# Column mean of an 8192 x 8192 matrix on one core: half-partition loads, slabs by row, and the last slab but one added on VectorE

## The chip, the cores and the metric

The kernel runs on one core of a Trainium2 chip. The metric is the time that the device takes for one execution, in microseconds (us). Lower is better.

## What is computed

```python
def setup_inputs():
    return {"x": np.random.randn(8192, 8192).astype(np.float32)}

def reference(x):
    return np.mean(x, axis=0)
```

The input is 268 MB of float32 and is read once; the output is one row of 8192 numbers. Each output is the sum of a column of 8192 rows, times 1/8192.

## The kernel before, in words

On-chip memory has 128 partitions. The matrix is cut into 64 slabs of 128 rows. Slabs 0 to 61 are taken as 31 pairs (`n_pairs`), one row of each slab per partition; slabs 62 and 63 are the tail.

**Pairs.** A tile `pair` holds 2 x 8192 columns on 128 partitions, and a pool has three such buffers (lines 41 and 93). In a pair's source, partition p holds the matrix rows 2p and 2p + 1 of the pair's 256 rows, which lie one behind the other in memory: 64 KB without a gap (line 94). Most pairs are one DMA of 8.4 MB. Pair 0 is cut after its first 2048 columns (`FIRST`), and the last three pairs (`BY_ROW = 3`, numbers 28 to 30) come in two DMAs, one for each of the two rows of a partition (lines 95 to 98). All loads are issued by SyncE (SP), in program order, onto one queue.

VectorE does two adds per pair (lines 99 to 102). The first adds the running sum, which stands in the first half of the pair before (`before`), to the first half of the new pair; this frees the older buffer. The second adds the new pair's second half. So the running sum moves along from buffer to buffer. A load into a buffer waits until the first add of the pair behind that buffer's old content is done. Each load signals through a semaphore, and the program has eight of these for loads, used in turn, so that a DMA also waits until the one eight places before it has landed.

**Tail.** The tail tile takes the pool's next buffer: slab 62 (`slab`) in its first half and slab 63 (`last`) in its second. Slab 62 comes in columns 0 to 4095 and 4096 to 7679 (`SPLIT`); its last 512 columns come as two loads of 120 and 8 partitions (`ROWS`, lines 112 and 113). Slab 63 comes in seven pieces of falling width (`PIECES`, line 116).

**The sum over partitions.** TensorE multiplies with a matrix of ones (128 x 32), which sums a column over the 128 partitions. The columns are dealt to PSUM banks: `WIDE` (three of 2048 and one of 1024 columns, each as four groups of a quarter) and `NARROW` (four of 256 columns). A bank collects from up to three sources: the running sum (`before`), slab 62 and slab 63. The first matmul of a bank has `start=True`, the last `stop=True`.

The second add of pair 30 is done in four parts of 2048 columns (lines 120 and 121), and VectorE adds slab 62's last 2048 columns to the last of these (line 123). The other three quarters of slab 62 go to TensorE (line 135). TensorE's order is written out by hand: for wide bank 0, 1, 2 the running sum and slab 62; wide bank 3 and the narrow banks from the running sum; then slab 63 for wide banks 0 to 3 (`close`, lines 139 and 140), each followed by a scaling on ScalarE (ACT); then slab 63 for the narrow banks, with scalings in turn on VectorE and ScalarE (lines 150 to 157). Three DMAs write the output: one from GpSimd (POOL) for the first 6144 columns, two from SP for the next 1024 and the last 1024.

The order on every engine is the order in the program (`manual_schedule`); no planner moves work.

Of the kernel before, what the change touches and what calls it, by code (L numbers as in the profile page):

```python
# [1 line left out]

# [4 lines left out]

F32 = mybir.dt.float32
ADD = mybir.AluOpType.add
GROUPS = 4  # L10

WIDE = (2048, 2048, 2048, 1024)
NARROW = (256, 256, 256, 256)
PIECES = (4096, 2048, 1024, 512, 256, 160, 96)
FIRST = 2048
BY_ROW = 3

ROWS = 120  # L20
SPLIT = 7680


@with_exitstack
def kernel(
    ctx: ExitStack,
    tc: tile.TileContext,
    x: bass.AP,
    out: bass.AP,
):  # L30
    nc = tc.nc
    P = nc.NUM_PARTITIONS
    R, C = x.shape
    n_slabs = R // P
    n_pairs = n_slabs // 2 - 1
    N0 = sum(WIDE)
    assert n_slabs % 2 == 0 and n_pairs >= 4 and N0 + sum(NARROW) == sum(PIECES) == C
    inv_r = 1.0 / float(R)

    const_pool = ctx.enter_context(tc.tile_pool(name="const", bufs=1))  # L40
    pair_pool = ctx.enter_context(tc.tile_pool(name="pair", bufs=3))
    psum_pool = ctx.enter_context(
        tc.tile_pool(name="acc", bufs=1, space=bass.MemoryType.PSUM)
    )
    res_pool = ctx.enter_context(tc.tile_pool(name="res", bufs=1))


    ctx.enter_context(tc.manual_schedule())

    ones = const_pool.tile([P, 32], F32)  # L50
    nc.gpsimd.memset(ones, 1.0)  # L51

    wide, lo = [], 0
    for n, w in enumerate(WIDE):
        bank = psum_pool.tile([P, w // GROUPS], F32, name=f"wide{n}", tag=f"wide{n}")
        wide.append((lo, w, bank))
        lo += w
    narrow = []
    for n, w in enumerate(NARROW):
        bank = psum_pool.tile([P, 512], F32, name=f"narrow{n}", tag=f"narrow{n}")  # L60
        narrow.append((lo, w, 32 * n, bank))
        lo += w

    def mm(dst, src, **flags):
        nc.tensor.matmul(out=dst, lhsT=ones, rhs=src, skip_group_check=True, **flags)  # L65

    def fold_wide(n, src, **flags):
        lo, w, bank = wide[n]
        q = w // GROUPS
        for g in range(GROUPS):  # L70
            a = lo + g * q
            mm(bank[32 * g : 32 * g + 32, :], src[:, a : a + q], **flags)

    def fold_narrow(n, src, lo, hi, **flags):
        at, _, g, bank = narrow[n]
        mm(bank[g : g + 32, lo - at : hi - at], src[:, lo:hi], **flags)

    def scaled(dst, src, eng):
        if eng == "act":
            nc.scalar.mul(out=dst, in_=src, mul=inv_r)  # L80
        else:
            nc.vector.tensor_scalar(  # L82
                out=dst, in0=src, scalar1=inv_r, scalar2=None, op0=mybir.AluOpType.mult
            )

    def add(dst, a, b):
        nc.vector.tensor_tensor(out=dst, in0=a, in1=b, op=ADD)  # L87

    before = None
    for k in range(n_pairs):
        pair = pair_pool.tile([P, 2 * C], F32, tag="pair")
        src = x[2 * P * k : 2 * P * (k + 1), :].rearrange("(p j) c -> p (j c)", j=2)
        cut = FIRST if k == 0 else C if k >= n_pairs - BY_ROW else 2 * C
        for lo, hi in ((0, cut), (cut, 2 * C)):
            if lo < hi:
                nc.sync.dma_start(out=pair[:, lo:hi], in_=src[:, lo:hi])  # L98
        if before is not None:
            add(pair[:, 0:C], pair[:, 0:C], before[:, 0:C])  # L100
        if k < n_pairs - 1:
            add(pair[:, 0:C], pair[:, 0:C], pair[:, C : 2 * C])
        before = pair


    tail = pair_pool.tile([P, 2 * C], F32, tag="pair")
    r = (n_slabs - 2) * P
    slab, last = tail[:, 0:C], tail[:, C : 2 * C]
    parts = [(lo, lo + w) for lo, w, _ in wide[:3]] + [(wide[3][0], C)]
    for lo, hi in ((0, C // 2), (C // 2, SPLIT)):  # L110
        nc.sync.dma_start(out=slab[:, lo:hi], in_=x[r : r + P, lo:hi])
    for a, b in ((0, ROWS), (ROWS, P)):
        nc.sync.dma_start(out=slab[a:b, SPLIT:C], in_=x[r + a : r + b, SPLIT:C])
    lo = 0
    for w in PIECES:
        nc.sync.dma_start(out=last[:, lo : lo + w], in_=x[r + P : R, lo : lo + w])
        lo += w


    for lo, hi in parts:  # L120
        add(before[:, lo:hi], before[:, lo:hi], before[:, C + lo : C + hi])
    lo, hi = parts[3]
    add(before[:, lo:hi], before[:, lo:hi], slab[:, lo:hi])

    rw = res_pool.tile([P, 3 * 512], F32, name="rw")
    r3 = res_pool.tile([P, WIDE[3] // GROUPS], F32, name="r3")
    row = res_pool.tile([1, C - N0], F32, name="row")

    def close(n):
        fold_wide(n, last, start=False, stop=True)  # L130
        scaled(rw[:, n * 512 : (n + 1) * 512] if n < 3 else r3, wide[n][2], "act")

    for n in range(3):
        fold_wide(n, before, start=True, stop=False)
        fold_wide(n, slab, start=False, stop=False)
    fold_wide(3, before, start=True, stop=False)
    for n, (lo, w, _, _) in enumerate(narrow):
        fold_narrow(n, before, lo, lo + w, start=True, stop=False)
    for n in range(4):
        close(n)  # L140
    W3 = 3 * GROUPS * 512
    nc.gpsimd.dma_start(  # L142
        out=out[0:W3].rearrange("(n g w) -> g n w", g=GROUPS, w=512),
        in_=rw.rearrange("(g r) (n w) -> g r n w", r=32, w=512)[:, 0],
    )
    nc.sync.dma_start(
        out=out[W3:N0].rearrange("(g w) -> g w", g=GROUPS),
        in_=r3.rearrange("(g r) w -> g r w", r=32)[:, 0],
    )
    for n, (lo, w, g, bank) in enumerate(narrow):  # L150
        if n < 3:
            fold_narrow(n, last, lo, lo + w, start=False, stop=True)
        else:
            cut = C - PIECES[-1]
            fold_narrow(n, last, lo, cut, start=False, stop=True)
            fold_narrow(n, last, cut, C, start=False, stop=True)
        scaled(row[0:1, lo - N0 : lo - N0 + w], bank[g : g + 1, 0:w], "act" if n % 2 else "dve")
    nc.sync.dma_start(out=out[N0:C], in_=row)


# [1 line left out]
_INS = ['x']  # L162
_OUTS = [((8192,), 'float32')]


# [23 lines left out]
```

## Time and profile before

| | |
|---|---|
| time, median of 3 runs | 629.22 us (628.69 to 629.66) |
| span of the profiled execution | 627.3 us |
| difference of the two | 1.9 us |
| read from memory | 268.44 MB, 428 GB/s over the span |
| load queue, share of 16 DMA engines' span | 99.2% |
| VectorE busy | 533.5 us (85%) |
| TensorE busy | 13.0 us (2%) |
| one add of 128 x 8192 | 8.692 us |
| one add of 128 x 2048 | 2.286 us |
| matmul records | 106, two for each matmul of the program |

The profiled execution has no time of its own apart from its span; the unprofiled runs' median lies 1.9 us above it. The profile names engines PE (TensorE), DVE (VectorE), ACT (ScalarE), POOL (GpSimd) and SP (SyncE). A group of instructions is shown with its line, its engine, its operation, the tiles that it writes and reads, its shape and its count; in square brackets stands how long the engine was idle before it and what ended that idle time. A table of stretches gives for each window the busy time of every engine, the clock granted to TensorE, the busy share of the DMA engines and the GB/s that they moved.

### The profile page before, as it was taken

Reading aid. Unit: us, or ns where it says so; the run is one execution under the profiler, and the core shown is the slowest. Engines: PE = TensorE matmul, PEld = TensorE weight load, DVE = VectorE, ACT = ScalarE, POOL = GpSimd, SP = SyncE. Lnnn points to the kernel's source line nnn. Section 1 sums busy time; section 2 is a strip of 40 time slices with the busy share of each in tenths; the row PEclk is TensorE's granted clock in tenths of the full one; section 3 lists DMA queues with packets and bytes.
Section 4 is the critical chain, followed back from the end, with each engine's and each line's share of the span. In section 5 each row is a group of like instructions: output and inputs, shape, how many; then the busy total and the mean of one; then the engine's idle time right before and its main releaser. Section 6 shows DMA issues by size and latency. Waiting matters only on the chain.

```text
span 627.3 us, 451 instructions
## 1 busy us (share of the span) xinstructions
PE 13.0 (2%) x106; PEld 3.8 (1%) x106; DVE 533.5 (85%) x67; ACT 4.2 (1%) x7; POOL 1.0 (0%) x6
## 2 busy tenths in 40 slices
PE   0000000000000000000000000000000000000016
PEld 0000000000000000000000000000000000000001
DVE  0538988889888899888898888988889888899994
ACT  0000000000000000000000000000000000000001
POOL 0000000000000000000000000000000000000000
PEclk9999999999999999999999999999999999999999
DMA  9999999999999999999999999999999999999997
GB/s 414 396 460 401 468 401 468 401 451 418 443 426 430 439 426 443 418 451 410 460 405 464 401 468 401 468 402 468 401 468 401 468 401 468 401 433 435 435 421 287
DMA packets 6548, 268.50 MB, mean 428 GB/s; under 512 B 900, under 2 KB 1160, under 8 KB 1553
## 3 DMA queue, kind: packets, MB, share of 16 engines
q1 hardware_dynamic: 6497, 268.45, 99.2%
q0 software_dynamic: 48, 0.02, 0.0%
q8 instruction: 1, 0.02, 0.0%
q14 instruction: 2, 0.02, 0.0%
HBM read 268.44 MB, written 0.03 MB: 428 GB/s over the span
## 4 chain that ended last, share of the span: by engine, by line
DMA 77%; DVE 22%; PE 0%; issue 0%; SPq 0%; ACT 0%; DVEq 0%
DMA pair<-in_x_dram 72%; DVE pair L87 22%; DMA tail<-in_x_dram 5%; PE narrow L65 0%; SPq L98 0%; PE wide L65 0%; ACT row L80 0%; DVEq L87 0%
## 5 line engine op out<-in xcount | busy, mean ns | idle before, releaser
L87 DVE TENSOR_TENSOR pair<-pair 128x8192 f32<-128x8192 f32 (+1 forms) x64 | 530.4, 8292 | 85.2 <-DMA pair<-in_x_dram 84.1
L65 PE MATMUL wide<-pair,ones 128*32 128x512 f32 (+1 forms) x32 | 4.8, 679 | 610.8 <-DVE pair L87 610.8
L65 PE MATMUL wide<-tail,ones 128*32 128x512 f32 (+1 forms) x56 | 7.7, 634 | 0.7 <-DMA tail<-in_x_dram 0.7
L82 DVE TENSOR_SCALAR row<-narrow 1x256 f32<-1x256 f32 x2 | 0.8, 416 | 6.2 <-PE narrow L65 6.1
L80 ACT ACTIVATE rw<-wide 128x512 f32<-128x512 f32 x3 | 1.8, 597 | 619.5 <-PE wide L65 619.5
L65 PEld LDWEIGHTS wide<-pair,ones 128*32 128x32 f32 x32 | 1.1, 134 | 613.5 <-issue 610.3
L87 DVE TENSOR_TENSOR pair<-pair,tail 128x2048 f32<-128x2048 f32 x1 | 2.3, 2292 | 0.0
L65 PEld LDWEIGHTS wide<-tail,ones 128*32 128x32 f32 x56 | 1.7, 119 | 6.1 <-issue 3.1
L142 POOL DMA_DIRECT2D out_dram<-rw x1 | 0.7, 695 | 622.7 <-ACT rw L80 622.7
L80 ACT ACT_TABLE_LOAD x1 | 1.3, 1283 | 0.7 <-PEq L173 0.7
L65 PE MATMUL narrow<-tail,ones 128*32 128x256 f32 (+2 forms) x10 | 1.2, 346 | 0.0
L80 ACT ACTIVATE row<-narrow 1x256 f32<-1x256 f32 x2 | 0.8, 376 | 0.4 <-PE narrow L65 0.2
L65 PEld LDWEIGHTS narrow<-tail,ones 128*32 128x32 f32 x10 | 0.6, 108 | 0.8 <-DMA tail<-in_x_dram 0.6
L65 PE MATMUL narrow<-pair,ones 128*32 128x256 f32 x8 | 0.6, 379 | 0.0
L80 ACT ACTIVATE r<-wide 128x256 f32<-128x256 f32 x1 | 0.4, 384 | 0.2 <-PE wide L65 0.2
L65 PEld LDWEIGHTS narrow<-pair,ones 128*32 128x32 f32 x8 | 0.3, 110 | 0.2
L51 POOL MEMSET ones<- 128x32 f32 x1 | 0.1, 124 | 0.3 <-POOLq L173 0.3
L173 POOL MEMSET const-float32-0.0<- 128x1 f32 x1 | 0.1, 98 | 0.2 <-issue 0.2
L173 POOL MEMSET const-float32-1.0<- 128x1 f32 x1 | 0.1, 98 | 0.0
L173 POOL MEMSET const-bfloat16-1.0<- 128x1 bf16 x1 | 0.1, 98 | 0.0
L173 POOL MEMSET const-uint8-127<- 128x1 uint8 x1 | 0.1, 98 | 0.0
## 6 DMA issues: line engine op xcount, KB each, us to landing
pair<-in_x_dram SPq DMA_DIRECT2D x6, 4096.0 KB, 25.8
pair<-in_x_dram SPq DMA_DIRECT2D x1, 7168.0 KB, 21.1
tail<-in_x_dram SPq DMA_DIRECT2D x2, 2048.0 KB, 19.2
tail<-in_x_dram SPq DMA_DIRECT2D x1, 1792.0 KB, 24.0
pair<-in_x_dram SPq DMA_DIRECT2D x1, 1024.0 KB, 4.7
tail<-in_x_dram SPq DMA_DIRECT2D x1, 1024.0 KB, 30.2
tail<-in_x_dram SPq DMA_DIRECT2D x1, 512.0 KB, 28.8
pair<-in_x_dram SPq DMA_DIRECT2D x27, 29.8
```

Of the source, the lines that this page charges most:

```text
L51: nc.gpsimd.memset(ones, 1.0)
L65: nc.tensor.matmul(out=dst, lhsT=ones, rhs=src, skip_group_check=True, **flags)
L80: nc.scalar.mul(out=dst, in_=src, mul=inv_r)
L82: nc.vector.tensor_scalar(out=dst, in0=src, scalar1=inv_r, scalar2=None, op0=mybir.AluOpType.mult)
L87: nc.vector.tensor_tensor(out=dst, in0=a, in1=b, op=ADD)
L142: nc.gpsimd.dma_start(out=out[0:W3].rearrange("(n g w) -> g n w", g=GROUPS, w=512), in_=rw.rearrange("(g r) (n w) -> g r n w", r=32, w=512 ...
L173: nc = _bacc.Bacc("TRN2", target_bir_lowering=False, num_devices=1)
```

## The change

- Pairs 0 to 24 are loaded in two DMAs, partitions 0 to 63 and 64 to 127; pair 0 in four, since it is still cut after 2048 columns.
- The last six pairs (25 to 30, `BY_ROW = 6`) are loaded slab by slab: partition p holds row p of the first slab and row p of the second. Pair 30 (`BY_HALF = 1`) comes in four loads of 4096 columns, and each of its two adds is done in two halves of 4096 columns.
- Slab 62 comes in two loads of 4096 columns on all 128 partitions. VectorE adds all of it to the running sum, in four parts of 2048 columns, and TensorE does not read it.
- Slab 63 comes in eight pieces; the first 4096 columns are now two pieces.
- The last narrow bank (256 columns) becomes two, of 160 and 96; the fifth narrow bank takes the PSUM place of wide bank 0 once that has been scaled. Its scaling is on VectorE.
- TensorE's 53 matmuls become 42, in another order: bank 0 from the running sum and from slab 63, then bank 1 the same, then bank 2, bank 3 and the narrow banks from the running sum, then slab 63 for the rest.

```diff
-NARROW = (256, 256, 256, 256)
-PIECES = (4096, 2048, 1024, 512, 256, 160, 96)
+NARROW = (256, 256, 256, 160, 96)
+PIECES = (2048, 2048, 2048, 1024, 512, 256, 160, 96)
 FIRST = 2048
-BY_ROW = 3
-
-ROWS = 120
-SPLIT = 7680
+BY_ROW = 6
+BY_HALF = 1
...
-    for n, w in enumerate(NARROW):
-        bank = psum_pool.tile([P, 512], F32, name=f"narrow{n}", tag=f"narrow{n}")
-        narrow.append((lo, w, 32 * n, bank))
-        lo += w
+    def open_narrow():
+        lo = N0
+        for n, w in enumerate(NARROW):
+            tag = f"narrow{n}" if n < GROUPS else "wide0"
+            bank = psum_pool.tile([P, 512], F32, name=f"narrow{n}", tag=tag)
+            narrow.append((lo, w, 32 * (n % GROUPS), bank))
+            lo += w
...
-        src = x[2 * P * k : 2 * P * (k + 1), :].rearrange("(p j) c -> p (j c)", j=2)
-        cut = FIRST if k == 0 else C if k >= n_pairs - BY_ROW else 2 * C
-        for lo, hi in ((0, cut), (cut, 2 * C)):
-            if lo < hi:
-                nc.sync.dma_start(out=pair[:, lo:hi], in_=src[:, lo:hi])
-        if before is not None:
-            add(pair[:, 0:C], pair[:, 0:C], before[:, 0:C])
-        if k < n_pairs - 1:
-            add(pair[:, 0:C], pair[:, 0:C], pair[:, C : 2 * C])
+        r = 2 * P * k
+        step = C
+        if k >= n_pairs - BY_ROW:
+            if k >= n_pairs - BY_HALF:
+                step = C // 2
+            for j in range(2):
+                for lo in range(0, C, step):
+                    nc.sync.dma_start(
+                        out=pair[:, j * C + lo : j * C + lo + step],
+                        in_=x[r + j * P : r + j * P + P, lo : lo + step],
+                    )
+        else:
+            src = x[r : r + 2 * P, :].rearrange("(p j) c -> p (j c)", j=2)
+            for lo, hi in ((0, FIRST), (FIRST, 2 * C)) if k == 0 else ((0, 2 * C),):
+                for a in (0, P // 2):
+                    b = a + P // 2
+                    nc.sync.dma_start(out=pair[a:b, lo:hi], in_=src[a:b, lo:hi])
+        for lo in range(0, C, step):
+            if before is not None:
+                add(pair[:, lo : lo + step], pair[:, lo : lo + step], before[:, lo : lo + step])
+        for lo in range(0, C, step):
+            add(pair[:, lo : lo + step], pair[:, lo : lo + step], pair[:, C + lo : C + lo + step])
...
-    for lo, hi in ((0, C // 2), (C // 2, SPLIT)):
+    for lo, hi in ((0, C // 2), (C // 2, C)):
         nc.sync.dma_start(out=slab[:, lo:hi], in_=x[r : r + P, lo:hi])
-    for a, b in ((0, ROWS), (ROWS, P)):
-        nc.sync.dma_start(out=slab[a:b, SPLIT:C], in_=x[r + a : r + b, SPLIT:C])
...
     for lo, hi in parts:
-        add(before[:, lo:hi], before[:, lo:hi], before[:, C + lo : C + hi])
-    lo, hi = parts[3]
-    add(before[:, lo:hi], before[:, lo:hi], slab[:, lo:hi])
+        add(before[:, lo:hi], before[:, lo:hi], slab[:, lo:hi])
...
-    for n in range(3):
-        fold_wide(n, before, start=True, stop=False)
-        fold_wide(n, slab, start=False, stop=False)
+    fold_wide(0, before, start=True, stop=False)
+    close(0)
+    fold_wide(1, before, start=True, stop=False)
+    close(1)
+    fold_wide(2, before, start=True, stop=False)
+    open_narrow()
     fold_wide(3, before, start=True, stop=False)
     for n, (lo, w, _, _) in enumerate(narrow):
         fold_narrow(n, before, lo, lo + w, start=True, stop=False)
-    for n in range(4):
-        close(n)
+    close(2)
+    close(3)
...
-        if n < 3:
-            fold_narrow(n, last, lo, lo + w, start=False, stop=True)
-        else:
-            cut = C - PIECES[-1]
-            fold_narrow(n, last, lo, cut, start=False, stop=True)
-            fold_narrow(n, last, cut, C, start=False, stop=True)
+        fold_narrow(n, last, lo, lo + w, start=False, stop=True)
```

## The prediction, made before the changed kernel had run

> **What bounds the kernel now.** I read the page's engine and DMA lines first, then VectorE's timeline, then a table of stretches, then the timeline of the last 20 us.
>
> ```profile
> PE 13.0 (2%) x106; PEld 3.8 (1%) x106; DVE 533.5 (85%) x67; ACT 4.2 (1%) x7; POOL 1.0 (0%) x6
> ...
> q1 hardware_dynamic: 6497, 268.45, 99.2%
> ...
> HBM read 268.44 MB, written 0.03 MB: 428 GB/s over the span
> ```
>
> The load queue keeps the 16 DMA engines busy for 99.2% of 627.3 us; VectorE (85%) is second. So a load that was merely late in being issued is not what costs time here; only the pace of the engines, and the two ends, can.
>
> ```profile
> 41.89 17.42 DVE L87 TENSOR_TENSOR pair<-pair 128x8192 f32<-128x8192 f32 x2 [10.76 <-DMA pair<-in_x_dram]
> 61.35 17.42 DVE L87 TENSOR_TENSOR pair<-pair 128x8192 f32<-128x8192 f32 x2 [2.04 <-DMA pair<-in_x_dram]
> ...
> 409.74 17.42 DVE L87 TENSOR_TENSOR pair<-pair 128x8192 f32<-128x8192 f32 x2 [1.85 <-DMA pair<-in_x_dram]
> 429.86 17.42 DVE L87 TENSOR_TENSOR pair<-pair 128x8192 f32<-128x8192 f32 x2 [2.70 <-DMA pair<-in_x_dram]
> ...
> 545.65 69.98 DVE L87 TENSOR_TENSOR pair<-pair 128x8192 f32<-128x8192 f32 x11 [1.89 <-DMA pair<-in_x_dram]
> 615.66 2.29 DVE L87 TENSOR_TENSOR pair<-pair,tail 128x2048 f32<-128x2048 f32 x1
> ```
>
> A line is a pair: two adds, 17.42 us, then a wait for the next landing. Starts lie 19.30 us apart in the steady part (8.39 MB each, 435 GB/s), a little more in the first six pairs (61.35 - 41.89 = 19.46; 0.9 us too much in all), and 20.12 us once, at 429.86. From 545.65 on VectorE never waits and ends at 617.95.
>
> ```profile
> 41.80:545.60 503.80, 0.00 (x0) 0.00 (x0) 451.98 (x52) 0.00 (x0) 0.00 (x0) 1.00 1.00 432
> ...
> 611.50:614.50 3.00, 3.00 (x28) 0.92 (x24) 3.00 (x2) 0.00 (x0) 0.00 (x0) 1.00 1.06 352
> ```
>
> The last two columns are the DMA share and GB/s. In 611.5 to 614.5 the engines are as busy as ever and move 352 GB/s: (432 - 352) x 3.0 us = 240 KB too little, 0.56 us. This is where the 120-row and 8-row loads (L113) run.
>
> ```profile
> 618.01 0.64 PE L65 MATMUL wide<-pair,ones 128*32 128x256 f32 x8 [1.66 <-DVE pair L87]
> 618.46 0.61 PE L65 MATMUL narrow<-pair,ones 128*32 128x256 f32 x8
> ...
> 622.82 0.64 PE L65 MATMUL wide<-tail,ones 128*32 128x256 f32 x8 [0.17 <-DMA tail<-in_x_dram]
> 623.44 1.16 PE L65 MATMUL narrow<-tail,ones 128*32 128x256 f32 x10
> ...
> 624.14 0.88 ACT L80 ACTIVATE row<-narrow 1x256 f32<-1x256 f32 x2 [0.23 <-PE narrow L65]
> ...
> 625.09 0.27 SPq L158 DMA_DIRECT2D out_dram<-row  x1
> ```
>
> TensorE is done with the pair at 619.1 and then waits for pieces of the last slab; from 622.8 everything follows the last landings.
>
> **Durations.** The DMA packet records of this execution, read one by one: 64 KB packets take 2.418 us (median of 3,456), 32 KB 1.213, 16 KB 0.611, 14 KB 0.535, 8 KB 0.309, 2 KB 0.084, and each engine's closing packet of a load 0.009. A full load is eight packets on each engine. The sum is made against the profiled execution, span 627.3; the median of the runs, 629.22, lies 1.9 us above it, and I carry that 1.9 over.
>
> **The change, part by part.**
>
> *Pairs 0 to 24 in two loads of 64 partitions.* If 64 partitions still spread over 16 engines (four packets each) at 2.418 us, only 26 more closing packets come in: 26 x 0.009 = +0.23. SP issues 26 more DMAs at 0.33 to 0.43 us, hidden: a slot's load is issued some 10 us before the stream reaches it (issue at 50.61, data from 61.3). Each half sits behind the other on one queue, and the wait for VectorE stands on the first half alone. What is not in the trace is 16 engines that write into 64 partitions only. Lower bound: nothing, or a gain up to the 0.9 us that the first pairs lose, since no row excludes that. Upper bound: the nearest row where rows and engines do not pair as in a full load, L113. Its 256 KB are 0.59 us of work at 435 GB/s and the stretch loses 0.56 us besides, so about twice the time; twice 19.30 for 25 pairs is +483 us. L113 may be slow for its odd row counts or its size instead: the 512-column piece of the last slab, also 2 KB packets, on 128 rows, shows 0.084 throughout. I take the low end, because four 64 KB packets per engine are nearest in size and queue to the 3,456 that ran at 2.418.
>
> [...]
>
> *Pairs 25 to 27 by row as well.* 16 packets of 1.213 for 8 of 2.418, one more closing packet: 3 x 0.073 = +0.22.
>
> *Pair 30 in quarters.* 32 x 0.611 for 16 x 1.213 and two closings: +0.16.
>
> *Slab 62 in two plain halves.* 16 x 0.611 = 9.78 for 8 x (0.611 + 0.535 + 0.084) = 9.84: -0.06, and the slow stretch goes, -0.56 (between 0, if it belongs to the place, and -0.56). One engine had been spared L113's share and now gets 0.61 back; it ends 0.25 to 0.5 us ahead of the others and 1.27 ahead of the last one (622.85 against 624.12), so 0.66 of cover is left.
>
> *Last slab's first piece in two:* 16 x 0.309 for 8 x 0.611: +0.07. The last four pieces are as before, each issued some 9 us before its data (its semaphore's earlier load, eight back, lands by 613.8).
>
> *VectorE.* It gains whole adds on slab 62 (three more 128x2048 of 2.29), and starts pairs 25 to 27 half a pair earlier. Replayed with 8.70 per add and 4.42 for 128x4096 (interpolated between 2.29 and 8.69): pair 24 lands at 487.7, adds run without a gap to 610.8, slab 62's four to 620.0, against 617.95. Four 256-column and five narrow matmuls then take 1.1 (rows at 618.01 to 619.07): 621.1. Wide 2's last four, on a piece that now lands at 621.54, take 0.43 to 0.86 (four weight loads step by 0.86 us at 610 and by 0.43 at 614), so 622.4 at the latest, before the 1024-column piece at 622.77. Counted from 621.1 the cover is 0.8 us; what VectorE is later than that goes one to one into the end.
>
> *Data order on TensorE.* Wide 0 and wide 1 are now closed before the pair's later parts are begun, so wide 1's start on the pair (VectorE's release at 615.4) waits behind wide 0's close on the last slab's first piece, about 616.7 (the 4096 columns land at 619.12, less 2.4 for 2048), and wide 2's start (617.7) behind the second piece at 619.12. ScalarE's scalings come earlier by this, and all of it ends before 621.1's work can: 0.
>
> *Eleven matmuls fewer* (twelve on slab 62 go, one narrow start comes; the trace counts each twice): they ran before 616, in the shade of the loads, 0. *Last scaling:* 96 columns on VectorE (under the 0.416 of 256) for 0.376 on ACT: 0 to -0.15, I take -0.1.
>
> *Instruction fetch.* The records show one 8 KB fetch of the instruction queue at 414.0 us; right after it one of the 16 engines lands 0.7 us late (the 20.12 step), and stays late to the end. More DMAs on SP may bring a second: 0 to +0.75, I take +0.3.
>
> Sum: 0.23 + 0.22 + 0.16 - 0.06 - 0.56 + 0.07 - 0.1 + 0.3 = +0.3, so 627.6 span, 629.5 us. Own range of this case, with the bounds above: 628.0 to 631.0.
>
> **The rivals.**
>
> *B, the lost steps go.* If halves read without the slow first pairs (-0.9) and the fetch falls where no engine is late (-0.8 and not +0.3), the end is 629.5 - 2.0 = 627.5. For it: both losses are in the trace and neither belongs to the work. Against: nothing in the change aims at the fetch.
>
> *C, two engines share one way into the 64 partitions, all along.* Place: every half load of pairs 0 to 24. Price: 25 x 19.3 = +483, 1112 us. It decides from the point where partners run in step, and engines do: they land within 0.3 us of each other. For it: L113's stretch. Against: every other packet of the trace runs at its engine's own pace, and that one odd load is the only witness.
>
> *D, they share but fall out of step.* Once one of two partners is a half load behind, they write to different halves and both run at full pace; the trailing one ends a half load (19.30 / 2 = 9.7 us) late: 639, and up to 649 if that takes twice as long to form.
>
> *E, VectorE ends too late.* If its replay is 1.5 us short, 0.8 of it covered, and TensorE stays at its slower pace (four 256-column, five narrow and four 512-column matmuls, some 0.9 more), about +1.5: 631. For it: its eleven adds in a row end only 5 us before the last landings. Against: the adds' length varies by 0.01 us.
>
> **How the numbers follow.** 0.2%, 1.26 us, is about what can be told from no change. Forecast A 0.42 (of it 0.05 faster, 0.27 same, 0.10 slower), B 0.15 faster, C 0.18, D 0.20 and E 0.05 slower. Faster 0.20, same 0.27, slower 0.53. The time is A's. C alone (0.18) is left out of the range: from B less the runs' scatter of 0.5 (627.0, taken as 626.8) to the end of D, 650.
>
> **What would show it.** Right: VectorE's pair starts 19.3 us apart from 61 to 490 us, 64 KB packets at 2.42, DMA at 430 GB/s or more in every stretch to 620, VectorE's last long add near 620.0, the last 256-column wide matmuls waiting for DMA. C: starts 38 us apart, packets near 4.8. D: the sixteen steps of a landing spread over 10 us. B: no 19.5 or 20.1 steps. E: a wait for VectorE ahead of the last wide matmuls. I am wrong above all if 64 partitions can't take what 16 engines bring.

## The result, and the profile after

The changed kernel takes 1159.26 us (median; 1158.16 to 1160.87), the kernel before, beside it, 628.96 us: a ratio of 1.8429, 95% interval 1.8407 to 1.8451. The forecast of 629.5 and its range to 650 were far off. Of the cases of the prediction rival C (1112 us) comes nearest; it had 0.18 and was the one case left out of the range.

VectorE's timeline of the changed kernel, columns as before (start, length, work, idle time ahead of it):

```profile
43.51 8.69 DVE L88 TENSOR_TENSOR pair<-pair 128x8192 f32<-128x8192 f32 x1 [43.51 <-DMA pair<-in_x_dram]
84.10 17.42 DVE L88 TENSOR_TENSOR pair<-pair 128x8192 f32<-128x8192 f32 x2 [31.90 <-DMA pair<-in_x_dram]
124.69 17.42 DVE L88 TENSOR_TENSOR pair<-pair 128x8192 f32<-128x8192 f32 x2 [23.17 <-DMA pair<-in_x_dram]
...
977.33 17.42 DVE L88 TENSOR_TENSOR pair<-pair 128x8192 f32<-128x8192 f32 x2 [23.17 <-DMA pair<-in_x_dram]
1018.24 95.96 DVE L88 TENSOR_TENSOR pair<-pair 128x8192 f32<-128x8192 f32 x11 [23.49 <-DMA pair<-in_x_dram]
```

The adds are as long as before, 17.42 us, but a pair now starts every 40.59 us (124.69 - 84.10) instead of every 19.30. At 1018.24 the last pair in halves has landed, and VectorE works for 96 us without a wait. The same point was 487.7 us before: 530.5 us are lost by then, all but 1.3 us of the difference between the two spans (1159.1 and 627.3).

The page's DMA lines and two stretches (the last two columns are the DMA share and GB/s):

```profile
q1 hardware_dynamic: 7626, 268.45, 99.5%
...
HBM read 268.44 MB, written 0.03 MB: 232 GB/s over the span
```

```profile
84.00:490.00 406.00, 0.00 (x0) 0.00 (x0) 173.84 (x20) 0.00 (x0) 0.00 (x0) 1.00 1.00 207
```

The load queue is 99.5% busy, as it was with 99.2%, and moves 207 GB/s. That is the trap in this column: "busy" is the time that packets were under way, and says nothing about their pace. The records of the single packets have the pace: a 64 KB packet takes 5.13 us (median of 3,072; the mean is 5.08) where it took 2.418. Behind pair 24, where loads cover 128 partitions again, 32 KB packets take 1.21 us, as before.

The other end of the timeline:

```profile
1146.19 1.93 PE L66 MATMUL wide<-tail,ones 128*32 128x512 f32 x8 [1.13 <-DMA tail<-in_x_dram]
...
1147.89 1.94 PE L66 MATMUL wide<-pair,ones 128*32 128x512 f32 x8
...
1149.60 1.93 PE L66 MATMUL wide<-tail,ones 128*32 128x512 f32 x8
...
1151.31 1.89 PE L66 MATMUL wide<-pair,ones 128*32 128x512 f32 x16
...
1154.78 0.90 PE L66 MATMUL narrow<-tail,ones 128*32 128x256 f32 x10
...
1156.75 0.28 SPq L166 DMA_DIRECT2D out_dram<-row  x1
```

TensorE no longer waits for the last pieces: from 1146.19 on it runs without a gap. The last piece lands at 1153.69 and the span ends at 1159.1, 5.4 us later; before, these were 624.12 and 627.3, 3.2 us.

### The profile page after: what moved, and what is told of

Read it like the earlier page. It is cut to its first block, busy times and chain, and to the rows that moved or that the text cites. A ratio compares the mean times of both kernels' runs of the same rounds, so it can differ in the third digit from the quotient of the medians.

```text
span 1159.1 us, 446 instructions
## 1 busy us (share of the span) xinstructions
PE 11.4 (1%) x84; PEld 3.6 (0%) x84; DVE 540.1 (47%) x70; ACT 4.0 (0%) x7; POOL 1.0 (0%) x6
## 3 DMA queue, kind: packets, MB, share of 16 engines
q1 hardware_dynamic: 7626, 268.45, 99.5%
## 4 chain that ended last, share of the span: by engine, by line
another core or an unknown queue 48%; DVE 44%; DMA 6%; PE 1%; issue 0%; SPq 0%; DVEq 0%
DVE pair L88 44%; DMA pair<-in_x_dram 4%; DMA tail<-in_x_dram 3%; PE wide L66 1%; SPq L111 0%; DVEq L88 0%; PE narrow L66 0%; SPq L125 0%; DVE row L83 0%; DVEq L192 0%
## 5 line engine op out<-in xcount | busy, mean ns | idle before, releaser
L88 DVE TENSOR_TENSOR pair<-pair,tail 128x2048 f32<-128x2048 f32 x4 | 8.9, 2282 | 0.0
```

## The experiments

### One part of the change alone, one part undone

Theory C, now mine: the engines write into 64 neighbouring partitions at half pace, wherever that part of the change stands. Rivals: it is the number or size of the loads, or another part of the change. e2_halves and e5_cols are the kernel before with one edit each; e1_whole is the changed kernel with one part undone. Here and below, where a cut of the code shows added lines alone, they stand in place of the one load line that e2_halves removes too.

```diff
 e2_halves, in the loop over the column ranges (lo, hi) of a pair:
-                nc.sync.dma_start(out=pair[:, lo:hi], in_=src[:, lo:hi])
+                for a, b in ((0, P // 2), (P // 2, P)) if k < n_pairs - BY_ROW else ((0, P),):
+                    nc.sync.dma_start(out=pair[a:b, lo:hi], in_=src[a:b, lo:hi])
 e5_cols:
+                m = (lo + hi) // 2
+                for a, b in ((lo, m), (m, hi)) if k < n_pairs - BY_ROW else ((lo, hi),):
+                    nc.sync.dma_start(out=pair[:, a:b], in_=src[:, a:b])
 e1_whole, from the changed kernel:
-                for a in (0, P // 2):
-                    b = a + P // 2
-                    nc.sync.dma_start(out=pair[a:b, lo:hi], in_=src[a:b, lo:hi])
+                nc.sync.dma_start(out=pair[:, lo:hi], in_=src[:, lo:hi])
```

> The kernel before with one part of the change alone: pairs 0 to 27 in two loads of 64 partitions. My theory (two engines that write into the same half of the partitions share one way and run in step, each at half pace) expects 40.6 us per pair for 28 pairs instead of 19.3: 629 + 28 x 21.3 = 1225 us, 64 KB packets at 5.13 us. If the slowness came from the other parts of the change (slabs by row, order of the tail): 629 to 632 us.

> The kernel before with pairs 0 to 27 in two loads of half the columns on all 128 partitions: as many loads as with the halves by partition, of the same 4 MB. My theory expects 19.3 to 19.4 us per pair and 628 to 632 us in all. If it is the number of loads or their size that costs, about 1200 us as with the halves.

> The changed kernel with pairs 0 to 24 as whole loads of 128 partitions again, all else as changed. By the two traces the changed kernel loses 530.5 us up to pair 24's landing (1018.2 against 487.7) and 1.3 us behind it, so 1159.3 - 530.5 = 628.8 in the runs, up to 630.3 by the span (627.3 + 1.3 + 1.9). I expect 630 us (629 to 631): TensorE, whose matmuls run without a gap at 0.86 us for four from 1146.2 to 1154.6 in the changed kernel, ends some 2 us after the last landing. If all of the loss came from the loads alone: 628.5 us or less, since the slow stretch of the 120-row load is gone.

Measured: e2_halves 1223.39 us, e5_cols 630.24 us (the kernel before beside them 629.33), e1_whole 629.45 us against 629.15, ratio 1.0004 (0.9995 to 1.0013). Stretches of e2_halves and of e5_cols:

```profile
60.00:500.00 440.00, 0.00 (x0) 0.00 (x0) 183.78 (x22) 0.00 (x0) 0.00 (x0) 1.00 1.01 207
```

```profile
60.00:500.00 440.00, 0.00 (x0) 0.00 (x0) 394.30 (x47) 0.00 (x0) 0.00 (x0) 1.00 1.00 433
```

The halves alone make the loss, and without them nothing measurable is left of the change. Number and size of the loads are not it: e5_cols has as many, of the same 4 MB.

### Reading or writing

A half load reads other addresses and writes other partitions than a full one. e4_even changes both: its two loads per pair take the even and the odd partitions. Then the two sides are crossed; the sum over the rows allows any pairing. e8_read_alt writes the slow way and reads as e4_even does, e9_write_alt the other way round. e12_quarters takes every fourth partition, so that a load has 32.

```diff
 e4_even:
+                for a, s in ((0, 2), (1, 2)) if k < n_pairs - BY_ROW else ((0, 1),):
+                    nc.sync.dma_start(out=pair[a::s, lo:hi], in_=src[a::s, lo:hi])
 e8_read_alt, against e2_halves:
+                    rows = src if b - a == P else src[2 * a // P :: 2, :]
+                    nc.sync.dma_start(out=pair[a:b, lo:hi], in_=rows[:, lo:hi])
 e9_write_alt, against e2_halves:
+                    parts_ = pair if b - a == P else pair[2 * a // P :: 2, :]
+                    nc.sync.dma_start(out=parts_[:, lo:hi], in_=src[a:b, lo:hi])
 e12_quarters:
+                for a, s in [(q, 4) for q in range(4)] if k < n_pairs - BY_ROW else [(0, 1)]:
+                    nc.sync.dma_start(out=pair[a::s, lo:hi], in_=src[a::s, lo:hi])
```

> The kernel before with pairs 0 to 27 in two loads of 64 partitions, the even ones and the odd ones, in place of the lower and the upper half. If what counts is which partitions a load reaches in all (even ones are spread over the whole range): packets near 2.42 us and 629 to 640 us. If what counts is which partitions the 16 engines write into at the same moment, and each engine has four neighbouring rows of the load, two engines may still meet: packets up to 5.1 us, up to 1225 us. If any load of 64 partitions is slow: 1225 us.

> Crosses the two sides of the load. Pairs 0 to 27 in two loads that write into partitions 0 to 63 and 64 to 127, as in the slow kernels, but read the even and the odd row pairs of the source, as the fast kernel with even and odd partitions did (the sum over rows does not care). If the write side is what is slow (where the engines write): about 1225 us, 64 KB packets at 5.1 us. If the read side is (which addresses the engines read at the same moment): 629 to 632 us, packets at 2.42.

> The other crossing: pairs 0 to 27 in two loads that write into the even and the odd partitions, and read the first and the second half of the pair's rows, as the slow kernels do. Write side: 629 to 632 us, packets at 2.42. Read side: about 1225 us, packets at 5.1.

> The kernel before with pairs 0 to 27 in four loads of 32 partitions each, every fourth partition. Theory N: an engine has two rows in its own eight partitions, nobody meets, 64 KB packets at 2.42, 629 to 634 us though a load has 32 partitions only. [...]

Measured, one run each: e4_even 631.27, e8_read_alt 1221.88, e9_write_alt 629.74, e12_quarters 632.25 us, with 629.1 to 629.4 for the kernel before beside them. The same stretch of e8_read_alt, then of e9_write_alt:

```profile
60.00:500.00 440.00, 0.00 (x0) 0.00 (x0) 184.26 (x22) 0.00 (x0) 0.00 (x0) 1.00 1.00 207
```

```profile
60.00:500.00 440.00, 0.00 (x0) 0.00 (x0) 394.99 (x47) 0.00 (x0) 0.00 (x0) 1.00 1.00 434
```

The pace goes with the partitions written, not with the addresses read. Nor is it that a load has few partitions: 32 of them, every fourth, go at 433 GB/s. e4_even and e12_quarters lose their 1.9 and 3.1 us in the first pair (VectorE's first add begins at 24.41 and 26.04 instead of 22.44) and none later.

### Which partitions are in each other's way

e10_rows puts extra loads with one row per engine ahead of the first pair, each kind into another set of partitions.

```diff
+    lead = pair_pool.tile([P, 2 * C], F32, tag="pair")
+    first = x[0 : 2 * P, :].rearrange("(p j) c -> p (j c)", j=2)
+    for top, s in ((P, 8), (64, 4), (32, 4), (64, 8), (P, 16)):
+        for q in range(4):
+            nc.sync.dma_start(out=lead[q:top:s, :], in_=first[q:top:s, :])
+    for lo in range(0, 2 * C, 4096):
+        nc.sync.dma_start(out=lead[0:8, lo : lo + 4096], in_=first[0:8, lo : lo + 4096])
     before = None
```

> The kernel before with extra loads ahead of the first pair (data not used), each row 64 KB, four loads of each kind: (a) 16 rows into every 8th partition, (b) 16 rows into every 4th of partitions 0 to 63, (c) 8 rows into every 4th of 0 to 31, (d) 8 rows into every 8th of 0 to 63, (e) 8 rows into every 16th, and (f) four loads of 16 KB rows into partitions 0 to 7. One engine has one row of a load. Theory N, neighbours: eight neighbouring partitions (number // 8) have one way in, at one engine's pace. Packets: (a) 2.42 us, (b) 4.8 to 5.1, (c) 4.8 to 5.1, (d) 2.42, (e) 2.42, (f) eight times 0.61, about 4.9. [...] The time of the whole is that of the kernel before and some 60 to 130 us more.

Measured, median of the packets in the records:

| load | us per packet | N expected |
|---|---|---|
| (a) 16 rows, every 8th partition | 5.09 | 2.42 |
| (b) 16 rows, every 4th of 0 to 63 | 5.10 | 4.8 to 5.1 |
| (c) 8 rows, every 4th of 0 to 31 | 2.42 | 4.8 to 5.1 |
| (d) 8 rows, every 8th of 0 to 63 | 5.10 | 2.42 |
| (e) 8 rows, every 16th | 5.10 | 2.42 |
| (f) 8 rows of 16 KB, partitions 0 to 7 | 2.40 | 4.9 |

The whole took 731.52 us, inside the 60 to 130 extra. Theory N, which had forecast e12_quarters rightly (632.25 us, of 629 to 634), falls in five of the six rows. Two rows say more: the eight partitions of (c) are not in each other's way (2.42 us), and (d)'s four in 0 to 31 are among them; with four more in 32 to 63, (d) takes 5.10 us. By these two rows, the crowd in (d) is between partitions 0 to 31 and 32 to 63. A grouping of all 128 partitions was not shown.

Nor do the partitions of a load decide alone: the 16 of (a), at 5.09 us, are half of the 32 that one load of e12_quarters covers, at 433 GB/s. I take it that what counts is which of them the engines write into at the same moment, and so which engine has which row. I had supposed neighbouring rows, and no record shows how the rows are dealt.

### Out of step

Rival D, and my reading of C, had the loss hang on partners running in step. Three kernels put engines out of step by extra loads ahead of e2_halves' first pair; e15_lone does one engine's load with nobody else at work, in the kernel before.

```diff
 e3_shift, e13_one, e14_two, against e2_halves (the rows of the extra loads differ, and each has one of the last three lines):
+    lead = pair_pool.tile([P, 2 * C], F32, tag="pair")
+    first = x[0 : 2 * P, :].rearrange("(p j) c -> p (j c)", j=2)
+    for q in range(4):
+        nc.sync.dma_start(out=lead[64 + q : 96 : 4, :], in_=first[64 + q : 96 : 4, :])   # e3_shift
+        nc.sync.dma_start(out=lead[124 + q : 125 + q, :], in_=first[124 + q : 125 + q, :])   # e13_one
+        nc.sync.dma_start(out=lead[60 + q : 128 : 64, :], in_=first[60 + q : 128 : 64, :])   # e14_two
 e15_lone, against the kernel before:
+        if k == 0:
+            for q in (124, 125, 126, 127, 0, 1, 2, 3):
+                nc.sync.dma_start(out=pair[q : q + 1, :], in_=src[q : q + 1, :])
```

> Pairs 0 to 27 in two loads of 64 partitions as before, and ahead of them four extra loads of 8 partitions x 64 KB (data that is not used), which should occupy eight of the 16 engines for one half load (4 x 2.42 = 9.7 us) and so put them one half load behind the others. My theory: partners now write to different halves, 64 KB packets fall from 5.13 us to near 2.42 us, pairs come every 19.3 to 25 us, the landing of one load spreads over about 10 us, and the whole takes 640 to 790 us. Rival: an engine is slow whenever its load covers 64 partitions, whatever the others do: packets stay near 5.1 us and the time is about 1225 + 10 = 1235 us; the same if the eight engines are not the partners of the other eight.

> Pairs 0 to 27 in two loads of 64 partitions, and ahead of them four extra loads of one row of 64 KB (data not used), which occupy one engine alone for 4 x 2.42 = 9.7 us and put it a half load behind all others. Theory of partners in step: this engine and its one partner then write to different halves and run at 2.42 us a packet as long as loads are queued (pairs 0 to 2, the first 60 to 100 us): 30 to 48 packets of 56 or 64 KB under 3.5 us, where the kernel with halves alone has none; later, when both have run ahead and wait for the next issue, they start it together and are in step again. Whole: about 1223 to 1235 us. If an engine is slow by itself whenever its load covers 64 partitions: no packet of the halves under 3.5 us beyond the four extra ones.

> The same with four extra loads of two rows, which occupy two engines (by the lowest numbers: 0 and 1) and put both a half load behind. If the partners are engines of neighbouring numbers: these two stay in step with each other and no packet of the halves, or only a handful at the start, is under 3.5 us. If the partners are eight numbers apart: two pairs of engines are relieved, 60 to 96 packets under 3.5 us.

> The kernel before with eight extra loads of one row of 64 KB ahead of pair 0, into partitions 124 to 127 and then 0 to 3, that end before any other load begins (pair 0 waits for them). One engine alone, nobody crowded. If the lone engine of e13_one went at 5.1 us only because the others were crowding the other half: 2.42 us for all eight, the whole 629 + 8 x 2.42 + about 3 = 651 to 655 us. If an engine is slow by itself into a way that is not its own: 5.1 us into partitions 124 to 127 and 2.42 into 0 to 3, about 662 us.

Measured: e3_shift 1246.40, e13_one 1242.83, e14_two 1253.29, e15_lone 650.25 us. In e3_shift eight engines' landings did stay some 12 us behind the other eight's (149.7 to 150.1 and 161.7 to 162.6 us, for instance), and the pace did not move. Two stretches of e3_shift, the first while the two groups write into different halves, the second while they write into the same:

```profile
150.00:162.00 12.00, 0.00 (x0) 0.00 (x0) 9.85 (x2) 0.00 (x0) 0.00 (x0) 1.00 1.06 218
162.00:170.00 8.00, 0.00 (x0) 0.00 (x0) 0.00 (x0) 0.00 (x0) 0.00 (x0) 1.00 0.95 197
```

(Packets are booked where they begin, hence shares off 1.00; divided by the share they are 206 and 207 GB/s.) This could still mean that both partners of every pair had been moved together. e13_one can't be read so: it moves one engine. I had expected 30 to 48 quick packets and found none: of the halves' packets not one took under 3.5 us, nor in e14_two. More, the lone engine's own four extra packets, into partitions 124 to 127, took 3.55, 5.91, 5.12 and 5.12 us. During the last two (11.1 to 21.4 us) all others were at 56 KB packets into the lower half, so nobody else wrote where this engine did. In e15_lone an engine with nobody beside it takes 3.13 us for the very first packet and 2.418 for each of the other seven, into 124 to 127 and 0 to 3 alike.

So the crowd comes from the write side (207 GB/s in e8_read_alt, 434 in e9_write_alt), and its pace, 5.13 us in place of 2.418, is also that of an engine that writes elsewhere at the time (5.12 us). Being out of step buys nothing, and D falls with it. What exactly backs up was not shown.

### The tail

Three kernels on the changed tail and on the two odd loads of the kernel before.

```diff
 e7_warm, against e1_whole:
+    warm = psum_pool.tile([P, 512], F32, name="warm", tag="narrow0")
+    for i in range(32):
+        g = 32 * (i % GROUPS)
+        mm(warm[g : g + 32, :], slab[:, 0:512], start=True, stop=True)
     fold_wide(0, before, start=True, stop=False)
 e11_warm2, against e1_whole:
+    def extra(count):
+        for i in range(count):
+            g = 32 * (i % GROUPS)
+            mm(warm[g : g + 32, :], before[:, C + 4096 : C + 4608], start=True, stop=True)
+    extra(28)   # warm: the same tile as in e7_warm
     fold_wide(0, before, start=True, stop=False)
+    extra(6)
 e6_plain, against the kernel before:
-    for lo, hi in ((0, C // 2), (C // 2, SPLIT)):
+    for lo, hi in ((0, C // 2), (C // 2, C)):
         nc.sync.dma_start(out=slab[:, lo:hi], in_=x[r : r + P, lo:hi])
-    for a, b in ((0, ROWS), (ROWS, P)):
-        nc.sync.dma_start(out=slab[a:b, SPLIT:C], in_=x[r + a : r + b, SPLIT:C])
```

> The kernel of e1_whole with 32 more matmuls (on slab 62's first 512 columns, into a bank that is opened afterwards, so the result does not use them) ahead of the first real ones, so that TensorE has been at work for some 5 us before VectorE's last adds arrive. If its slow pace comes from having been idle: 0.43 us for four from the first real matmul on, TensorE waits for the last pieces again, and the end comes 1 to 2.2 us earlier than in e1_whole: 628 to 629 us. If the pace does not depend on that: as e1_whole, 630 us or a little over.

> The kernel of e1_whole with 28 extra matmuls that start when pair 30's last quarter lands (about 604 us) and should end by 612.5, before VectorE's first quarter of the last adds, and six behind wide bank 0's first four; the result does not use them. A matmul of 512 columns takes 0.43 us at the slow pace and 0.215 at the fast one by e1_whole and e7_warm. If the late end is due to the slow pace: TensorE is done 0.3 us behind the last landing, 0.8 to 1.3 us earlier than in e1_whole, 628.2 to 628.7 us, a little faster than before. If it is due to the order (closing bank 0 and 1 early) or to the three scalings on VectorE: 629.4 us as e1_whole.

> The kernel before with slab 62 in two plain halves of 4096 columns, without the 120-row and the 8-row load. If these two cost 0.56 us in the slow stretch (eight engines that write into eight neighbouring partitions): the stretch at 611.5 to 614.5 us shows 430 GB/s, the last landings come 0.5 us earlier, 628.6 us. If the stretch belongs to the place and not to the loads: 629.2 us or, with the one engine that had been spared now as late as the others, up to 629.5.

Measured: e7_warm 629.96 against 629.15 us, ratio 1.0010 (1.0001 to 1.0019); e11_warm2 629.34 against 629.20, 1.0001 (0.9992 to 1.0010); e6_plain 627.88 against 629.20, 0.9983 (0.9974 to 0.9992).

e7_warm's extra matmuls were too many: they ran to 617.7, past VectorE's first quarter at 612.9, so TensorE still worked without a gap to the end. e11_warm2 has them earlier. TensorE at the last close, first in e1_whole, then in e11_warm2:

```profile
622.99 0.63 PE L66 MATMUL wide<-tail,ones 128*32 128x512 f32 x3
...
623.14 1.45 PE L66 MATMUL wide<-tail,ones 128*32 128x512 f32 x13
...
626.27 0.29 SPq L164 DMA_DIRECT2D out_dram<-row  x1
```

```profile
621.58 1.06 PE L66 MATMUL wide<-tail,ones 128*32 128x512 f32 x8 [0.25 <-DMA tail<-in_x_dram]
...
622.81 0.64 PE L66 MATMUL wide<-tail,ones 128*32 128x256 f32 x8 [0.16 <-DMA tail<-in_x_dram]
...
625.28 0.28 SPq L173 DMA_DIRECT2D out_dram<-row  x1
```

With the extra work TensorE waits for the pieces again, and the last output is issued 1.0 us earlier although the last piece landed 0.6 us later (624.11 against 623.54). The mechanism is there; the medians of the runs, 629.34 and 629.45, do not show it, and the 628.2 to 628.7 expected of it were missed. The profiled run of e1_whole was one of its slowest (630.52, of 628.32 to 630.55), so how late TensorE is seems to differ from run to run; that is argued, not shown.

e6_plain's stretch, to lay beside the 352 GB/s of the kernel before:

```profile
611.50:614.50 3.00, 3.00 (x27) 0.77 (x20) 3.00 (x2) 0.00 (x0) 0.00 (x0) 1.00 1.02 437
```

The slow stretch belongs to the 120-row and 8-row loads: without them the last piece lands at 622.87 instead of 624.12. Some 0.4 us of that was there by pair 27 already (545.21 against 545.65). This one edit is faster than the kernel before by 1.3 us (0.5 to 1.6 by the interval).

## Why the prediction was wrong

**The step that failed** is the price of the 64-partition loads. I had bounded it by "nothing" and by twice the time, from the one row where rows and engines pair otherwise (L113), and took the low end, "because four 64 KB packets per engine are nearest in size and queue to the 3,456 that ran at 2.418". Size and queue were the wrong likeness. All 3,456 packets belong to loads of 128 partitions, so none of them could speak about 64. The measured factor is 40.59 / 19.30 = 2.10 between pair starts, from packets of 5.13 us in place of 2.418; the upper end had 2, which is why C's 1112 us is short of 1159. C had the place and nearly the price, but not the mechanism: it let the loss hang on partners in step, and e13_one shows that it does not.

**The other evidence was weighed and not followed.** L113's stretch was the one row with a price for C, about twice the time, and I gave the case 0.18 because "that one odd load is the only witness". One row where rows and engines pair otherwise is more than 3,456 that cannot see the question.

**Why L113 was slow** was left as size or odd row counts, and is still open. e10_rows (f) suggests a reason: eight engines into eight neighbouring partitions go at four times the packet time (2.40 us against 0.611 for 16 KB). But the packet records of the kernel before put only 0.06 us per engine of the loss into L113's own 2 KB packets (0.084 to 0.245 us each). The other 0.55 us are in the load right behind, on all 128 partitions: its first 16 KB packet took 0.98 to 1.08 us on 15 of the 16 engines, where e6_plain has 0.611 throughout. Whether these wait for the crowd of the eight rows was not tested. So L113 was no row of 64 partitions either, and that its stretch gave nearly the right factor is in part luck.

**Right, by its steps:** the rest of the change. e1_whole, the changed kernel without the halves, measures 629.45; the forecast for loads at full pace was 629.5. That the two agree to 0.05 us is luck, since two errors below cancel. VectorE's replay had it done at 620.0; e1_whole has 619.4, the changed kernel 1149.6, which is 619.1 after the 530.5 are taken off. The second instruction fetch came (records at 863.9 and 996.3 us, where there was one).

**Right in sign, off in size:** slab 62 in plain halves, -0.6 in the sum, is -1.3 in e6_plain. That gain pays for the tail: from e6_plain's 627.88 to e1_whole's 629.45 the other parts of the change cost 1.6 us, and the sum had 0.65 for them.

**Wrong and hidden by that:** TensorE's tail. I read four weight-load records in 0.86 us as four matmuls; every matmul has two records, as the front of this document says, so four cost 1.71 us at the slow pace and 0.86 at the fast one. The TensorE half of rival E (0.05) came true in the profile: the end lies 5.4 instead of 3.2 us behind the last landing. Its other half did not, as VectorE is 0.6 us early by e1_whole and not late. (The expectations of e1_whole and e7_warm still have the halved times, 0.86 and 0.43 us for four matmuls.) The profile's granted clock reads 1.00 all through these stretches, so the two paces can't be read from that column. The pace doubled 3.8 us after the first matmul in the kernel before, and not before 6.0 us after TensorE's last wait, at 1146.2, in the changed one. What sets that moment was not shown.

**D** fell: partners out of step do not recover the pace. **B** was not seen: the 20.1 step is still there in e1_whole (429.79 - 409.76 = 20.03).

**The range** left C out because it was alone at 0.18. With two bounds so far apart and one witness, its chance should have been above 0.2, and the range would have had to reach it.

## What to carry to other kernels

Ask of every load which partitions it writes, not only how many bytes per row: in these runs 64 neighbouring partitions halved the pace of all 16 DMA engines (207 GB/s, e2_halves), while every second or every fourth of all 128 ran at 434 and 433 GB/s (e4_even, e12_quarters), as whole loads do (432 in the kernel before). Spreading alone does not do it: 16 rows into every eighth partition were as slow as the halves (e10_rows (a), 5.09 us). A DMA share near 1.00 is no sign of a load at full pace (it stood beside 207 and beside 434 GB/s); read GB/s or packet times beside it. When a cost has bounds far apart, do not choose by many rows that all lack the property that is changed, here the partitions; if no row has it, keep both bounds in the range.

## What was not expected of the hardware

- One engine that writes where nobody else does goes at 5.12 us per 64 KB while the others crowd one half, and at 2.418 alone.
- The crowd costs a packet a factor of 2.10 to 2.12 (5.09 and 5.13 us against 2.418), not 2. Why is open.
- Loads of 32 partitions, every fourth, run at 433 GB/s once past the first pair.
- Two small loads of 256 KB in all, L113, cost a whole kernel some 1.3 us (0.5 to 1.6) by the runs. The packet records place 0.6 us of it, nearly all in the load behind them.
